# The fixed instruction order lifted from an attention and convolution mixer

## The chip, the cores and the metric

The kernel runs on one core of a Trainium2 chip. The metric is the device time of one execution in microseconds, taken as the median of several runs. The engines are named as in the profile: PE (TensorE matmuls; PEld is its weight load), DVE (VectorE), ACT (ScalarE), POOL (GpSimd), SP (SyncE). Each engine executes its own queue strictly in the order in which it was written; between engines there are semaphores.

## The reference

A decoder trunk of two layers on one sequence of 512 tokens, width 1024. Each layer is a feed-forward block, a mixer and another feed-forward block. The mixer of layer 0 is the part that this change touches. Cut to it:

```
h = h + 0.5 * swiglu_ffn(rms_norm(h, ffn1_norm[l]), ...)
h = h + hybrid_mixer(rms_norm(h, mix_norm[l]), cos, sin, ...)      # layer 0
h = h + 0.5 * swiglu_ffn(rms_norm(h, ffn2_norm[l]), ...)

def hybrid_mixer(h, cos, sin, w_in, dw_w, dw_b, ln_g, ln_b, w_out):
    proj = h @ w_in                                   # q, k, v: 512 each; u: 2 x 512
    q, k = apply_partial_rotary(q), apply_partial_rotary(k)    # 8 heads of 64
    # three dilated causal windows per head, mixed by their softmax denominators
    attn = einsum(softmax(lses), outs)
    glu = u[..., :512] * sigmoid(u[..., 512:])
    c = causal_depthwise_conv(glu, dw_w) + dw_b       # 31 taps
    c = silu(layer_norm(c, ln_g, ln_b))
    return concatenate([attn, c]) @ w_out
```

Layer 1 has a gated DeltaNet mixer instead, and all is float32.

## The kernel before

Activations lie transposed: 128 channels on the partitions, 512 tokens along a row, eight such tiles for the width. Every float32 matmul is done as three (L140 to L142, `mm3`): each operand is split into a high and a low part, and high x high, high x low and low x high are added in PSUM.

Weights come by `load_split`: SP issues the load into `raw`, ACT copies it to `whi` (L126) and writes its negative to `wlo` (L127), and POOL issues a DMA (L128) that adds the source onto `wlo`, so that `wlo` is the low part when this DMA has landed. There are four `raw` buffers and three pairs `whi`/`wlo`. The feed-forward blocks have a second form of this (L116 on ACT, L117 on DVE).

The mixer of layer 0 runs from about 393 to 697 us of the span, in this order of writing:

- Four rounds of two projections for the convolution's input. Within the first, the norm's row factors are made: `stats`, `scale` (a reciprocal root on DVE, L147 to L152), `rows` (L156 on PE, copied by ACT to `R`, L288). The angles of the rotation follow (`angles`: L751 to L757 on DVE, two Sin on ACT).
- Four quarters of the projection of V.
- `raw_rows` projects one head pair's q or k (24 matmuls; ACT copies the result to `qa`, L852, and DVE multiplies it by the cosine to `u`, L854). `rotate` swaps halves with a matmul (`tr`, L860), DVE multiplies by the sine and adds (L862, L863), ACT and DVE split into high and low (`qh`/`ql`, `kh`/`kl`; L865, L866).
- For each of four head pairs t: `scores` makes eight blocks of scores (`sc`, L881 to L883, 128 to 512 columns), DVE takes mask and maximum of each (L886), ACT the exponential (L887) and the division (L893). `values` transposes the probabilities (L913), ACT copies them to `pt` (L916), PE multiplies by V (L921). The values of head pair t-1 are written between the projections and rotations of t+1, ahead of the scores of t.
- The causal convolution runs on DVE: 4 channel tiles of 31 taps each, 124 instructions (L774, L778) of the tiles `cv`. `taps(n)` writes the next n of them at places chosen by hand: 5 at each projection, 7 at each quarter of V, 4 or 8 in `raw_rows`, 5 after the scores.
- `layer_norm` of the convolution is written in steps between the rotations, values and scores of the last head pair: sum on DVE (L926 to L928), mean by a matmul (L929), variance (L939, L942), then the scale, a Silu on ACT (L957) and a split.
- The out-projection: parts of the first three output tiles (attention's first inputs) are written ahead of the last values, the rest (`out_mm`) after them. `ahead` writes the first weights of the next feed-forward block in between, and `nxt.feed` makes the next norm's statistics and splits.

What sets the order: in most of the kernel, this mixer included, the instructions of PE, ACT and DVE are under a manual schedule, so that each of these engines executes them as written. PSUM has two banks for each of the names `mm`, `sc`, `tr`, `po`; a third score block therefore waits for the maximum of the first. The DeltaNet mixer of layer 1 is not under a manual schedule. The functions that the change touches, with the profile's line numbers:

Of the kernel before, what the change touches and what calls it, by code (L numbers as in the profile page):

```python
# [50 lines left out]
def trunk(ctx, tc, io, out, phases):  # L51
    nc = tc.nc
# [44 lines left out]
    def psum(tag):  # L97
        return pp.tile([P, T], F32, tag=tag, name=nm(tag))
# [215 lines left out]
    def step(ahead):  # L314
        if ahead is not None:
            next(ahead, None)
# [394 lines left out]
        return take, early()  # L711

    def hybrid(xn, nxt, ahead, take):
        with tc.tile_pool(name="ho", bufs=1, side="right", reuse_waits="tile") as op, \
                tc.manual_schedule(engines={nc.tensor.engine, nc.scalar.engine, nc.vector.engine}):
            with tc.tile_pool(name="hy", bufs=1, side="right", reuse_waits="tile") as hp:
                o_x, ps = hybrid_heads(xn, op, hp, take)
            xn.close()
            nxt.open()
            for d in range(NK):  # L720
                if d < 3:
                    out_mm(ps[d], take(20 + d), o_x, (4, 5, 6, 7, 3), False, True)
                else:
                    ps[d] = psum("po" if d % 2 else "mm")
                    wt = take(20 + d)
                    for _ in range((0, 0, 0, 0, 0, 0, 1, 1)[d]):
                        step(ahead)
                    out_mm(ps[d], wt, o_x, range(NK), True, True)
                V.tensor_add(h[d], ps[d], h[d])
                nxt.feed(d)  # L730
                for _ in range((0, 0, 0, 0, 0, 0, 2, 2)[d]):
                    step(ahead)
            nxt.fed()

    def out_mm(ps, wt, xs, ks, first, last):
        for k in ks:
            hi, lo = wt[k // 4]
            c = slice(k % 4 * P, k % 4 * P + P)
            mm3(ps, hi[:, c], lo[:, c], xs[k], first and k == ks[0], last and k == ks[-1])
# [614 lines left out]
    for i, ph in enumerate(phases):  # L1354
        if ph == "m_0":
            hybrid(xs[i], xs[i + 1], stages[i + 1], take)
        elif ph == "m_1":
            gdn(xs[i], xs[i + 1], stages[i + 1])
        else:
            try:  # L1360
                stages[i].send((xs[i + 1], stages[i + 1]))
            except StopIteration:
                pass
# [90 lines left out]
```

## Time and profile before

| | |
|---|---|
| median of 3 runs | 2170.47 us (2166.86 to 2171.05) |
| the profiled execution | 2171.57 us |
| its span | 2169.8 us |
| its mean granted TensorE clock | 0.961 |
| PE / DVE / ACT / POOL busy | 94% / 75% / 51% / 6% |
| the mixer of layer 0 | about 393 to 697 us of the span |

The span is the time from the first to the last instruction of one profiled execution. A row of the timeline has the start, the length, the engine, the line, the operation with its output and inputs, and in brackets how long the engine stood before it and what released it. A row of the waits has how long an engine stood for one kind of releaser in total, how often, and the longest.

### The profile page before, as it was taken

The page shows a single profiled execution, that of the slowest core. Times are in us where ns is not written, and L with a number is a line of the kernel's source. Part 1 is how long each engine was busy: PE and PEld are TensorE (multiplying, and loading weights), DVE is VectorE, ACT ScalarE, POOL GpSimd, SP SyncE. Part 2 cuts the span into 40 slices and gives each one's busy share as a digit, 9 for nine tenths or more (in the row PEclk, how much of TensorE's full clock was granted, in tenths as well). Part 3 has the DMA queues.
Part 4 walks back from the last instruction along what each step waited for, and adds up shares of the span by engine and source line. Part 5 has one row for each costly group of instructions (what it writes and reads, how often), then busy time and mean ns, then how long its engine had stood idle before and what let it go on. Part 6 is the DMA issues. An engine that isn't in the chain of part 4 may idle for free.

```text
span 2169.8 us, 32960 instructions
## 1 busy us (share of the span) xinstructions
PE 2034.5 (94%) x12694; PEld 1799.4 (83%) x12694; DVE 1624.2 (75%) x2758; ACT 1117.0 (51%) x1981; POOL 133.8 (6%) x190
## 2 busy tenths in 40 slices
PE   7999999997678999999899999998989999999997
PEld 6999997774446999997799999776778888999986
DVE  5888778786536788789888887865765568888876
ACT  5444447444444444446544445676535664444455
POOL 0000000110000000000000000033402220000000
PEclk9999999997779999999999999999979999999999
DMA  3333333772104333332233332379836453333331
GB/s 121 105 101 109 101 100 104 166 168 52 39 20 121 98 100 110 98 98 78 93 107 98 107 107 89 110 219 230 194 100 151 107 122 113 103 107 98 103 93 44
DMA packets 108845, 237.70 MB, mean 110 GB/s; under 512 B 22160, under 2 KB 24976, under 8 KB 108688
## 3 DMA queue, kind: packets, MB, share of 16 engines
q1 hardware_dynamic: 90544, 193.06, 29.0%
q0 software_dynamic: 17616, 42.02, 10.5%
q8 instruction: 99, 1.62, 0.3%
q10 hardware_dynamic: 528, 0.52, 0.1%
q14 instruction: 58, 0.48, 0.1%
HBM read 224.55 MB, written 11.01 MB: 109 GB/s over the span
## 4 chain that ended last, share of the span: by engine, by line
PE 74%; DVE 11%; issue 9%; ACT 3%; DMA 3%; POOL 0%; SPq 0%; DVEq 0%; POOLq 0%; ACTq 0%
PE mm L141 11%; PE mm L142 11%; PE mm L140 11%; PE sc L141 7%; PE sc L140 7%; PE sc L142 7%; PE po L142 2%; PE po L141 2%; PE po L140 2%; PE tr L140 2%; PE tr L142 2%; PE tr L141 2%; DVE cv L778 1%; DVE wlo L117 1%; DVE gl L386 1%
## 5 line engine op out<-in xcount | busy, mean ns | idle before, releaser
L117 DVE TENSOR_TENSOR wlo<-raw,whi 128x1024 fp32r<-128x1024 f32 (+1 forms) x400 | 473.1, 1201 | 161.0 <-ACT whi L116 156.6
L140 PE MATMUL mm<-xh,whi 128*128 128x256 f32 (+2 forms) x1800 | 562.9, 313 | 8.6 <-ACT b L456 4.0
L142 PE MATMUL mm<-xh,wlo 128*128 128x256 f32 (+2 forms) x1800 | 558.2, 310 | 7.6 <-DMA wlo<-in_whyb 4.3
L141 PE MATMUL mm<-xl,whi 128*128 128x256 f32 (+2 forms) x1800 | 557.2, 310 | 0.0
L116 ACT ACTIVATE whi<-raw 128x1024 fp32r<-128x1024 f32 (+1 forms) x400 | 404.5, 1033 | 31.1 <-issue 14.4
L140 PEld LDWEIGHTS mm<-xh,whi 128*128 128x128 f32 (+1 forms) x1800 | 344.5, 191 | 43.5 <-ACT b L456 7.2
L141 PEld LDWEIGHTS mm<-xl,whi 128*128 128x128 f32 (+1 forms) x1800 | 344.7, 191 | 26.3 <-issue 0.5
L142 PEld LDWEIGHTS mm<-xh,wlo 128*128 128x128 f32 (+1 forms) x1800 | 344.7, 192 | 24.7 <-DMA wlo<-in_whyb 5.1
L140 PE MATMUL sc<-xh,whi 128*128 128x256 f32 x1056 | 301.6, 286 | 13.2 <-ACT whi L116 5.6
L141 PE MATMUL sc<-xl,whi 128*128 128x256 f32 x1056 | 300.1, 284 | 2.2 <-DVE xl L251 2.2
L142 PE MATMUL sc<-xh,wlo 128*128 128x256 f32 x1056 | 300.3, 284 | 1.8 <-DVE wlo L117 1.7
L140 PEld LDWEIGHTS sc<-xh,whi 128*128 128x128 f32 x1056 | 203.5, 193 | 15.7 <-DVE b L458 6.2
L141 PEld LDWEIGHTS sc<-xl,whi 128*128 128x128 f32 x1056 | 203.5, 193 | 2.7 <-DVE xl L251 2.7
L142 PEld LDWEIGHTS sc<-xh,wlo 128*128 128x128 f32 x1056 | 203.6, 193 | 2.5 <-DVE wlo L117 2.5
L386 DVE TENSOR_TENSOR gl<-g,gh 128x512 fp32r<-128x512 f32 (+1 forms) x286 | 178.5, 643 | 32.3 <-ACT gh L385 29.9
L385 ACT ACTIVATE gh<-g 128x512 fp32r<-128x512 f32 (+1 forms) x286 | 166.3, 592 | 67.1 <-PE mm L141 34.7
L403 ACT ACTIVATE a<-a 128x512 f32<-128x512 f32 x88 | 55.6, 632 | 253.9 <-DVE a L402 253.9
L442 ACT ACTIVATE b<-mm 128x256 f32<-128x256 f32 x84 | 32.1, 383 | 155.9 <-PE mm L142 155.9
L126 ACT ACTIVATE whi<-raw 128x512 fp32r<-128x512 f32 (+2 forms) x109 | 76.7, 732 | 58.8 <-PE mm L141 36.5
L456 ACT ACTIVATE b<-mm 128x256 f32<-128x256 f32 x88 | 33.6, 382 | 139.5 <-PE mm L142 139.5
L778 DVE SCALAR_TENSOR_TENSOR cv<-pad,prm_t,cv 128x512 f32<-128x512 f32 x120 | 90.1, 751 | 4.1
L141 PE MATMUL mm<-gl,whi 128*128 128x512 f32 (+1 forms) x220 | 83.0, 377 | 4.8 <-DVE gl L386 4.6
(419 smaller groups left out, 3567.2 us busy)
## 6 DMA issues: line engine op xcount, KB each, us to landing
raw<-in_wf1i SPq DMA_DIRECT2D x82, 512.0 KB, 3.5
raw<-in_wf2i SPq DMA_DIRECT2D x82, 512.0 KB, 3.5
raw<-in_wgdn SPq DMA_DIRECT2D x32, 512.0 KB, 4.2
wlo<-in_wgdn POOLq DMA_DIRECT2D x64, 256.0 KB, 6.0
raw<-in_wf2i SPq DMA_DIRECT2D x56, 256.0 KB, 2.6
raw<-in_wf1i SPq DMA_DIRECT2D x52, 256.0 KB, 2.6
raw<-in_wf1b SPq DMA_DIRECT2D x20, 512.0 KB, 3.5
raw<-in_wf2b SPq DMA_DIRECT2D x20, 512.0 KB, 3.5
```

What stands on the lines that cost most here:

```text
L116: A.activation(hi[:, s], src[:, s], AF.Copy)
L117: V.tensor_sub(lo[:, s], src[:, s], hi[:, s].bitcast(F32))
L126: A.activation(hi[:, s], raw[:, s], AF.Copy)
L140: PE.matmul(ps, whi, xhi, start=first, stop=False, skip_group_check=skip)
L141: PE.matmul(ps, whi, xlo, start=False, stop=False, skip_group_check=skip)
L142: PE.matmul(ps, wlo, xhi, start=False, stop=last, skip_group_check=skip)
L385: A.activation(hi, g[f][:, s], AF.Copy)
L386: V.tensor_sub(lo, g[f][:, s], hi.bitcast(F32))
L403: A.activation(cg[f], cg[f], AF.Silu)
L442: A.activation(b0[f][:, HT:], pb[f][:, :HT], AF.Copy)
L456: A.activation(b1[f][:, :HT], pb[f][:, :HT], AF.Copy)
L778: V.scalar_tensor_tensor(acc, x, w, acc, op0=ALU.mult, op1=ALU.add)
```

## The change

The `hybrid` function enters two contexts: a pool, and the manual schedule for the three engines. The second is dropped; the scheduler now orders the instructions of the mixer on these engines, from the same written sequence. The feed-forward blocks stay under their manual schedules.

```
     def hybrid(xn, nxt, ahead, take):
-        with tc.tile_pool(name="ho", bufs=1, side="right", reuse_waits="tile") as op, \
-                tc.manual_schedule(engines={nc.tensor.engine, nc.scalar.engine, nc.vector.engine}):
+        with tc.tile_pool(name="ho", bufs=1, side="right", reuse_waits="tile") as op:
             with tc.tile_pool(name="hy", bufs=1, side="right", reuse_waits="tile") as hp:
                 o_x, ps = hybrid_heads(xn, op, hp, take)
```

From this line on, line numbers are one lower than before. Each engine has the same instructions; on PE 284 change their place, on DVE 315, on ACT 163, on POOL none, and on SP two pairs of loads swap.

VectorE, from the last score maximum of head pair 0 to the rotation behind it. `cv` are convolution taps, `tr_799` is the swapped key of head pair 1, `rd` a reciprocal of the softmax's denominators. Before:

```order
L886 ISA s3_790_4848,m_791_4849<-sc_789_4844,hcst_4054 128x512
L886 ISA m_791_4849 128x1
L891 RECIPROCAL rd_767_4782<-den_765_4780 128x4
L778 SCALAR_TENSOR_TENSOR cv_747_4704<-pad_684_4258,prm_t_67,cv_747_4704 128x512 x13
L854 TENSOR_TENSOR u_798_4905<-mm_796_4870,Ct_653_4060 128x512
L862 TENSOR_TENSOR t1_800_4909<-tr_799_4907,St_654_4061 128x512
L863 TENSOR_TENSOR u_759_4768<-u_759_4768,t1_800_4909 128x512
L866 TENSOR_TENSOR kl_802_4913<-u_759_4768,kh_801_4912 128x512
```

And now:

```order
L885 ISA s3_790_4846,m_791_4847<-sc_789_4842,hcst_4052 128x512
L885 ISA m_791_4847 128x1
L777 SCALAR_TENSOR_TENSOR cv_813_4971<-pad_695_4338,prm_t_67,cv_813_4971 128x512 x3
L890 RECIPROCAL rd_767_4780<-den_765_4778 128x4
L861 TENSOR_TENSOR t1_800_4907<-tr_799_4905,St_654_4059 128x512
L853 TENSOR_TENSOR u_798_4903<-mm_796_4868,Ct_653_4058 128x512
L862 TENSOR_TENSOR u_759_4766<-u_759_4766,t1_800_4907 128x512
L777 SCALAR_TENSOR_TENSOR cv_813_4971<-pad_695_4338,prm_t_67,cv_813_4971 128x512 x2
L865 TENSOR_TENSOR kl_802_4911<-u_759_4766,kh_801_4910 128x512
```

Thirteen taps stood between the maximum and the rotation, and three stand there now; they are of the fourth channel tile (`cv_813`) instead of the third, since the earlier ones are already done. Ahead of these rows, taps of two tiles alternate in the new order, where a tile's taps followed each other before. Counted up to the first score maximum of head pair 0, 78 of the 124 taps stood ahead before and 99 now; between the last row of the first rotated key (`kl_753`) and that maximum there were eight taps, and there are four. All 124 stand ahead of the rotated key of head pair 2 (`kl_866`) now, and the LayerNorm sum (L926) stands among the scores of head pair 2 instead of behind them.

TensorE at the scores of head pair 0. `sc_768`, `sc_771`, `sc_774`, `sc_777` are the first four score blocks, `mm_796` the projection of the next query. Before:

```order
L881 MATMUL sc_771_4791<-kh_752_4722,qh_741_4668 128x256
L882 MATMUL sc_771_4791<-kl_753_4723,qh_741_4668 128x256
L883 MATMUL sc_771_4791<-kh_752_4722,ql_742_4669 128x256
L881 MATMUL sc_774_4799<-kh_752_4722,qh_741_4668 128x384
L882 MATMUL sc_774_4799<-kl_753_4723,qh_741_4668 128x384
L883 MATMUL sc_774_4799<-kh_752_4722,ql_742_4669 128x384
L881 MATMUL sc_777_4807<-kh_752_4722,qh_741_4668 128x512
```

And now:

```order
L882 MATMUL sc_771_4789<-kh_752_4720,ql_742_4667 128x256
L140 MATMUL mm_796_4868<-xh_512_3534,whi_744_4672 128x512
L141 MATMUL mm_796_4868<-xl_513_3535,whi_744_4672 128x512
L142 MATMUL mm_796_4868<-xh_512_3534,wlo_745_4673 128x512
L140 MATMUL mm_796_4868<-xh_522_3573,whi_744_4672 128x512
L141 MATMUL mm_796_4868<-xl_523_3574,whi_744_4672 128x512
L142 MATMUL mm_796_4868<-xh_522_3573,wlo_745_4673 128x512
L140 MATMUL mm_796_4868<-xh_538_3630,whi_744_4672 128x512
L141 MATMUL mm_796_4868<-xl_539_3631,whi_744_4672 128x512
L880 MATMUL sc_774_4797<-kh_752_4720,qh_741_4666 128x384
```

The eight score blocks followed each other, and then came the 24 matmuls of the projection; now eight of these stand behind the second block, four behind the fourth, two behind the sixth, and ten behind the last. The transposes of the probabilities (L913, now L912) are interleaved with the next projection in the same way: two of its matmuls behind the first group, six behind the second. In head pairs 2 and 3 parts of the out-projection take the projection's place.

ScalarE at the out-projection's first weight (`whi_981`, `wlo_982`). Before:

```order
L893 ACTIVATE s3_974_5511<-s3_974_5511,rd_951_5445 128x512
L952 ACTIVATE t1_978_5526<-tr_977_5521 128x512
L126 ACTIVATE whi_981_5535<-raw_980_5533 128x1024
L127 ACTIVATE wlo_982_5536<-whi_981_5535 128x1024
L957 ACT_TABLE_LOAD
L957 ACTIVATE cv_677_4209<-cv_677_4209,prm_t_67 128x512
```

And now:

```order
L915 ACTIVATE pt_872_5172<-tr_871_5169 128x256
L126 ACTIVATE whi_981_5533<-raw_980_5531 128x1024
L851 ACTIVATE qa_877_5218<-mm_876_5185 128x512
L127 ACTIVATE wlo_982_5534<-whi_981_5533 128x1024
L915 ACTIVATE pt_884_5236<-tr_883_5231 128x512
```

It stood behind the last divisions of the last head pair, and now stands among the copies of the transposed probabilities two head pairs earlier, 51 instructions before. At the front, DVE's angles (L750 to L756 now) alternate with the reciprocal root, eight more matmuls of the second projection stand ahead of the transposes of the row factors on PE, the two Sin ahead of the copy to `R` on ACT, and the splits of the second round's weights (`whi_680`) ahead of the gate's tanh. At the end, the splits of the last output tiles' weights and of the next feed-forward block's first weights stand ahead of the squares and splits of `nxt.feed`.

## The prediction

> **What bounds the kernel now.** First the page: where the span ends and who fills it.
>
> ```profile
> span 2169.8 us, 32960 instructions
> PE 2034.5 (94%) x12694; PEld 1799.4 (83%) x12694; DVE 1624.2 (75%) x2758; ACT 1117.0 (51%) x1981; POOL 133.8 (6%) x190
> ...
> L778 DVE SCALAR_TENSOR_TENSOR cv<-pad,prm_t,cv 128x512 f32<-128x512 f32 x120 | 90.1, 751 | 4.1
> ```
>
> TensorE (PE) sets the end of the span, and an average of 94% leaves 135 us in which it stood. The change touches one phase of six, so I looked next at the stretches of that phase, busy time and granted clock side by side.
>
> ```profile
> 425.00:479.00 54.00, 54.00 (x236) 44.17 (x235) 40.14 (x56) 24.11 (x27) 7.77 (x9) 0.99 0.79 177
> 479.00:650.00 171.00, 122.86 (x427) 81.63 (x426) 93.05 (x191) 78.43 (x164) 5.18 (x6) 0.75 0.18 41
> 650.00:700.00 50.00, 39.80 (x171) 31.41 (x170) 33.33 (x54) 25.20 (x30) 4.32 (x5) 0.95 0.44 95
> ```
>
> The columns are length, then busy time of PE, PEld, DVE, ACT and POOL, then the granted clock. While the projections run (425 to 479) PE is full at clock 0.99, one matmul every 0.23 us (54.00 / 236), and VectorE (DVE) has 13.9 us free. In the attention part (479 to 650) PE stands 171 - 122.86 = 48.1 us, and its busy time runs at 0.75: 122.86 x 0.25 = 30.7 us lost to the clock, 92.1 us of work at full speed. No engine is full there; the stretch is made of waits. The waits of PE from 393 to 720 name them (total, times, longest):
>
> ```profile
> PE sc L881 <- DVE m L886: 14.3, 7, 8.8
> PE tr L913 <- DVE t L862: 10.3, 4, 4.9
> PE sc L929 <- DVE t L928: 7.3, 1, 7.3
> PE tr L913 <- ACT pt L916: 6.9, 9, 1.2
> PE sc L140 <- ACT whi L116: 5.6, 1, 5.6
> PE sc L142 <- DMA wlo<-in_whybo: 5.1, 1, 5.1
> PE mm L142 <- DMA wlo<-in_whyb: 4.3, 2, 4.1
> PE tr L942 <- DVE t L939: 4.2, 1, 4.2
> PE po L142 <- DMA wlo<-in_whybo: 3.5, 1, 3.5
> PE sc L142 <- DVE wlo L117: 1.0, 1, 1.0
> ```
>
> Rows 1 to 4, 6 and 8 add up to 48.1, the whole idle time of 479 to 650. The front has 4.3, the out-projection 3.5, the next phase's start 5.6 + 1.0.
>
> **The change, part by part.** No instruction is added or removed; three engines run the same ones in another order. So every term is a wait that shrinks, grows or appears.
>
> *Scores of head pair 0 and the second rotation.* The rows of DVE, and PE beside them:
>
> ```profile
> 485.72 6.26 DVE L778 SCALAR_TENSOR_TENSOR cv<-pad,prm_t,cv 128x512 f32<-128x512 f32 x8
> 491.90 0.68 DVE L854 TENSOR_TENSOR u<-mm,Ct 128x512 f32<-128x512 f32 x1
> 492.50 0.68 DVE L862 TENSOR_TENSOR t<-tr,St 128x512 f32<-128x512 f32 x1
> ...
> 495.56 0.68 PE L881 MATMUL sc<-kh,qh 64*128 64x384 f32 x1 [8.76 <-DVE m L886]
> ...
> 504.31 10.17 DVE L778 SCALAR_TENSOR_TENSOR cv<-pad,prm_t,cv 128x512 f32<-128x512 f32 x13
> 514.40 0.68 DVE L854 TENSOR_TENSOR u<-mm,Ct 128x512 f32<-128x512 f32 x1
> ...
> 515.73 1.11 PE L913 MATMUL tr<-cst,s 128*128 128x128 f32 x4 [4.04 <-DVE t L862]
> ```
>
> Eight convolution taps in a row stand ahead of the rotation and the first score maximum, and PE waits 8.76 us for the maximum to free a score bank. In the new order four of those taps stand there: 4 x 0.78 = 3.1 us earlier. Eight matmuls of the next projection, 1.8 us at 0.23 each, fill part of the rest. All told 99 taps instead of 78 are done by then, 21 x 0.75 = 15.8 us more work, but DVE has that room earlier (13.9 us free in 425 to 479 alone, some 3 us around it) and its taps now alternate between two channels: 13 chained taps took 10.17 (0.78 each), while neighbours that don't depend on each other started 0.60 apart (491.90 to 492.50). Of that 0.18 I count 0.115 for each of some 50 taps, since a tap lasts 0.07 longer than those neighbours: 6 us, of which about 2.5 land on this wait. So 8.76 - 3.1 - 1.8 - 2.5 = 1.3 us remain; bounds 0 and 8.8. The other six of the seven (5.5 us) I cut to a third, 1.8, since matmuls of the projection stand between the score blocks there too: 14.3 becomes 3.1.
>
> Thirteen taps then hold up the rotation that PE waits 4.04 for (4.9 in the next head pair). Three stand there now: ten fewer, 7.8 us, more than the wait. Each drops to about 0.5; with the two small ones 10.3 becomes 2.0. VectorE's queue behind the taps (the score maxima, and ScalarE's exponentials that wait for them) comes forward with it.
>
> PE's nine waits on ScalarE for transposed probabilities (L916), of at most 1.2 us each, are covered by matmuls of the next projection that now stand between the transposes: two or more at 0.23 each time, and six behind the second group. 6.9 becomes 1.9.
>
> The Trainium skill, "VectorE: DVE Perf Modes", section "The DRAIN you can't avoid", has it that the next operation starts only when the pipeline has emptied and that leaving out semaphores gains nothing; by that, alternating channels saves none of the 6 us and the forecast would be 6 us higher. The trace shows 0.78 against 0.60 apart, so it disagrees for these shapes.
>
> *The convolution's LayerNorm.*
>
> ```profile
> 585.35 3.08 DVE L778 SCALAR_TENSOR_TENSOR cv<-pad,prm_t,cv 128x512 f32<-128x512 f32 x4
> 588.35 0.68 DVE L926 TENSOR_TENSOR t<-cv,cv 128x512 f32<-128x512 f32 x1
> ...
> 590.54 2.08 PE L929 MATMUL sc<-t,hcst 128*128 128x512 f32 x2 [7.29 <-DVE t L928]
> ```
>
> The last four taps stand behind all scores, and PE waits 7.29 for the sum. They are now done before the scores of that head pair, the sum inside them: 0. The variance's 4.2 falls to 0.3 with it.
>
> *The tail and the weights of the out-projection.*
>
> ```profile
> 626.51 1.92 ACT L893 ACTIVATE s<-s,rd 128x128 f32<-128x128 f32 x4 [0.25 <-DVE rd L891]
> ...
> 628.81 1.05 ACT L126 ACTIVATE whi<-raw 128x1024 fp32r<-128x1024 f32 x1
> ...
> 630.97 1.28 ACT L957 ACT_TABLE_LOAD   x1
> ...
> 631.24 0.86 POOL L128 DMA_DIRECT2D wlo<-in_whybo  x1 [70.05 <-ACT wlo L127]
> ...
> 632.26 0.81 ACT L957 ACTIVATE cv<-cv,prm_t 128x512 f32<-128x512 f32 x1
> 633.11 0.63 ACT L134 ACTIVATE hi<-cv 128x512 fp32r<-128x512 f32 x1
> ...
> 636.44 0.79 PE L142 MATMUL sc<-hi,wlo 128*128 128x512 f32 x1 [5.08 <-DMA wlo<-in_whybo]
> ```
>
> ScalarE splits this weight at 628.81, POOL's DMA follows and lands 5.2 us after its issue. The split now stands 51 instructions earlier, two score blocks ahead, so the 5.1 us go. POOL's and SP's queues carry nothing else at that time (0.86 us of issue), so moving the transfer collides with nothing. In exchange PE has already done the parts of the out-projection that filled this place, and comes earlier to the first part that needs the convolution's output. That part waits for normalising, table load, Silu and split: 1.92 + 1.28 + 0.81 + 0.63 = 4.6 plus small steps, bounds 0 and 5.2; I take 4.3, near the whole chain, since nothing is left to put there. The scores of the last head pair now start as soon as their keys are rotated: a chain like 492.50 to 495.56 (3.1 us), of which I take 1.8, and 1.2 for the next two score blocks, bounds 0 and 4.9 (the longest wait for a rotation now). New waits: 7.3.
>
> *Front.* The angles of the rotation (L751 to L757) are now interleaved with the reciprocal root that the row factors need:
>
> ```profile
> 398.53 0.42 DVE L751 CAST qa<-qa 128x512 f32<-128x512 int32 x1
> ...
> 402.61 0.43 DVE L757 TENSOR_SCALAR qa<-qa 128x512 f32<-128x512 f32 x1
> ```
>
> They take 4.5 us, and at worst all of that goes in front of the factors. Eight matmuls of the second projection now stand ahead of the factors' transposes on PE and hide 1.8; one of the two Sin ahead of the factors' copy on ScalarE adds 0.6 (a 128x512 activation, as at 633.11). I take 4.5 - 1.8 + 0.6 = 3.3 of new wait. Against it the weights' splits stand ahead of that chain on ScalarE and the 4.3 of the wait for a weight's DMA go: a gain of 1.0, bounds -4.5 and +4.3.
>
> *Out-projection and start of the next phase.* The remaining weight splits stand ahead of the feed's squares and splits on ScalarE. 3.5 becomes 2.1 and 5.6 + 1.0 becomes 1.0, a gain of 7.0, bounds 0 and 10.1.
>
> *The clock.*
>
> ```profile
> 495.00:508.00 13.00, 11.93 (x33) 9.48 (x34) 7.76 (x24) 11.02 (x27) 0.00 (x0) 0.52 0.00 1
> 534.00:546.00 12.00, 10.97 (x40) 8.25 (x39) 6.89 (x23) 9.49 (x26) 0.00 (x0) 0.72 0.00 1
> 576.00:591.00 15.00, 6.96 (x26) 5.22 (x26) 9.65 (x26) 9.12 (x25) 0.00 (x0) 0.61 0.00 0
> ...
> 535.97 0.44 PE L881 MATMUL sc<-kh,qh 64*128 64x384 f32 x1 [0.74 <-DVE m L886]
> ```
>
> The clock is low after the long waits, but also in 534 to 546, where the longest wait was 0.74. So I don't give back all of the 30.7: in proportion to the idle time that is left. That is 3.1 + 2.0 + 1.9 + 0.3 + 7.3 = 14.6 of 48.1, or 30%: 9.3 stay lost, 21.4 are gained. The Trainium skill, "TensorE: Matmul & The Clock Gate", section "HAM oscillation — how this bites in real kernels", puts half clock down to idle gaps longer than about 3.4 us; only one wait of that size would be left, and by that rule nearly all 30.7 come back (the second rival's time).
>
> **Sum.** 1.0 (front) + 33.5 (48.1 - 14.6) + 21.4 (clock) + 7.0 = 62.9. The profiled execution took 2171.57 us (span 2169.8 and 1.8 around it): 2108.7. It lies 1.1 above the median of the runs, 2170.47, so I predict 2107.6.
>
> **The rivals.** *VectorE becomes the bound.*
>
> ```profile
> 398.00:588.30 190.30, 154.98 (x599) 114.27 (x597) 137.57 (x233) 85.80 (x148) 15.54 (x18) 0.86 0.45 102
> ```
>
> Up to the LayerNorm sum it is busy 137.57 of 190.3 us, 72%. My sum needs some 38 of the gains before 588, so about 90% busy without the alternation, 86% with it. If it reaches only 80%, the sum comes at 570 instead of 588: 18.0, and behind it 3.9 + 2.3 + 5.1 + 7.0 - 5.5 = 12.8. That gives 2171.57 - 30.8 - 1.1 = 2139.7. For it speaks that taps still precede score maxima in an engine that runs in order.
>
> *The clock comes back whole.* If matmuls that follow each other closely are enough to hold 0.99 here as in 425 to 479, the 9.3 are gained too: 2098.3; with the new waits at their lower bounds some 7 less, 2091. Against it speaks 534 to 546.
>
> *Slower: the clock stays down.* The new order puts small score and transpose matmuls (64 rows, 128 to 512 columns) between the projection's full ones, so there may be no stretch left that restores the clock. The 92.1 us of work plus 14.6 of waits, less 8.0 from front and end, equal today's 171 at clock 92.1 / 164.4 = 0.56; below that the change costs. At the 0.52 of 495 to 508 it gives 92.1 / 0.52 + 14.6 - 8.0 - 171 = 12.7 more: 2183. Against it: the projections hold 0.99.
>
> *Nothing measurable.* Waits taken away on PE could reappear behind DVE's taps, since the taps are only moved; that needs every term to be paid back, and would give 2170.
>
> **Chances.** The forecast (2100 to 2115) 0.40, VectorE bound or half of the gain (2115 to 2155) 0.28, the clock whole (2082 to 2100) 0.16, slower 0.12, nothing 0.04. A difference under 0.2% (4.3 us) can't be told from none on this kernel. Range 2082 to 2150, which leaves out the last two and the far end of the second; faster 0.84, same 0.04, slower 0.12.
>
> **What would show it.** In the new profile: the waits of L880 for the maximum and of L912 for L861 below 1.5 us each; no wait of L928; a wait of 2 to 5 us of the out-projection's matmul for the Silu's split; granted clock about 0.9 in the attention stretch; DVE near 90% busy from 400 on. Wrong would be: DVE late at the first maximum, the clock at 0.75 with few waits, or a PE wait well over 3.3 us on the row factors around 398, which would mean that the angles weigh more than taken.

## The result and the profile after

The changed kernel takes 2098.93 us (median of 3 runs, 2097.34 to 2100.03), against 2170.47: ratio 0.9674, 95% interval 0.9652 to 0.9696. The prediction was 2107.6, in a range of 2082 to 2150. The profiled execution has a span of 2097.2 us, 72.6 less than before.

The page after, where the span ends and who fills it:

```profile
span 2097.2 us, 32970 instructions
...
PE 2020.4 (96%) x12694; PEld 1785.7 (85%) x12694; DVE 1609.0 (77%) x2758; ACT 1113.9 (53%) x1981; POOL 134.0 (6%) x190
```

To compare the two traces I cut them at the same instructions of PE: the statistics of the mixer's norm (L271), the first score matmul, and the first matmul of the next phase. The two stretches of before, and then those of after; the columns are length, busy time of PE, PEld, DVE, ACT and POOL, and the granted clock:

```profile
392.53:485.85 93.32, 88.66 (x384) 71.21 (x382) 73.37 (x115) 39.72 (x45) 12.09 (x14) 0.98 0.73 164
485.85:690.77 204.92, 153.22 (x558) 106.08 (x557) 112.65 (x225) 97.25 (x187) 9.50 (x11) 0.79 0.23 52
```

```profile
390.90:479.34 88.44, 86.81 (x383) 70.15 (x381) 85.89 (x143) 41.62 (x48) 13.07 (x15) 1.00 0.79 184
479.34:621.78 142.44, 138.28 (x557) 91.33 (x557) 90.72 (x200) 92.90 (x187) 8.64 (x10) 0.93 0.32 71
```

The front became 4.9 us shorter, the stretch from the scores through the out-projection 62.5 us. The rest is 3.6 us behind it and 1.6 us in the unchanged first phase (the same instructions end there at 390.90 instead of 392.53; in the traces of the kernels below that have the same first phase they lie anywhere between 390.5 and 392.8, so this part can't be put down to the change). Together that is the 72.6. In the long stretch PE's idle time went from 51.7 to 4.2 us, its busy time from 153.2 to 138.3 and its clock from 0.79 to 0.93. VectorE shows where its work went: 12.5 us more of it in the front, 21.9 us less behind.

The waits of PE from 479 to 650 in the changed kernel, to be read against the ten rows of before:

```profile
PE mm L140 <- ACT hi L134: 1.2, 1, 1.2
PE sc L141 <- DVE xl L251: 1.1, 1, 1.1
PE po L142 <- DMA wlo<-in_whybo: 1.0, 1, 1.0
...
PE sc L880 <- ACT kh L864: 0.7, 1, 0.7
...
PE sc L880 <- DVE m L885: 0.5, 2, 0.3
...
PE tr L912 <- ACT pt L915: 0.2, 1, 0.2
```

The score maximum (14.3 before) is down to 0.5, the rotation, the LayerNorm sum and the variance aren't in the list any more, and among the new waits are the two that were named: the Silu's split (1.2) and the last rotated key (0.7). At the start of the next phase the 5.6 + 1.0 for a weight have become 1.1 + 0.5 for the split of that phase's input (`xl`, `xh`).

VectorE's timeline at the first scores:

```profile
476.85 2.73 DVE L777 SCALAR_TENSOR_TENSOR cv<-pad,prm_t,cv 128x512 f32<-128x512 f32 x4
479.50 0.68 DVE L861 TENSOR_TENSOR t<-tr,St 128x512 f32<-128x512 f32 x1
480.10 0.68 DVE L853 TENSOR_TENSOR u<-mm,Ct 128x512 f32<-128x512 f32 x1
480.69 0.68 DVE L862 TENSOR_TENSOR u<-u,t 128x512 f32<-128x512 f32 x1
481.29 0.28 DVE L885 CUSTOM_DVE_ANT_0 s<-sc,hcst 128x128 f32<-128x128 f32 x1
...
482.51 0.68 DVE L865 TENSOR_TENSOR ql<-u,qh 128x512 fp32r<-128x512 f32 x1
```

The first maximum starts at 481.29, 1.95 us after the first score matmul (479.34). Before it was 9.4 us after it (495.21 against 485.85). Before, all of the next query's rotation stood ahead of the maxima, its split (L866) included; now the split stands behind two of them.

### The profile page after: what moved, and what is told of

Read it like the earlier page. It is cut to its first block, busy times and chain, and to the rows that moved or that the text cites. A ratio compares the mean times of both kernels' runs of the same rounds, so it can differ in the third digit from the quotient of the medians.

```text
span 2097.2 us, 32970 instructions
## 1 busy us (share of the span) xinstructions
PE 2020.4 (96%) x12694; PEld 1785.7 (85%) x12694; DVE 1609.0 (77%) x2758; ACT 1113.9 (53%) x1981; POOL 134.0 (6%) x190
## 4 chain that ended last, share of the span: by engine, by line
PE 80%; DVE 8%; issue 5%; ACT 3%; DMA 3%; SPq 0%; POOL 0%; DVEq 0%; ACTq 0%; POOLq 0%
PE mm L141 13%; PE mm L140 13%; PE mm L142 13%; PE sc L141 7%; PE sc L140 7%; PE sc L142 7%; PE po L142 3%; PE po L141 2%; PE po L140 2%; PE tr L140 2%; PE tr L142 2%; PE tr L141 2%; DVE wlo L117 1%; DVE gl L386 1%; PE tr L1051 1%
## 5 line engine op out<-in xcount | busy, mean ns | idle before, releaser
L117 DVE TENSOR_TENSOR wlo<-raw,whi 128x1024 fp32r<-128x1024 f32 (+1 forms) x400 | 473.3, 1201 | 158.8 <-ACT whi L116 154.3
L116 ACT ACTIVATE whi<-raw 128x1024 fp32r<-128x1024 f32 (+1 forms) x400 | 404.8, 1034 | 33.9 <-issue 14.4
L777 DVE SCALAR_TENSOR_TENSOR cv<-pad,prm_t,cv 128x512 f32<-128x512 f32 x120 | 83.8, 743 | 0.8
```

Source lines behind the costliest of these rows:

```text
L116: A.activation(hi[:, s], src[:, s], AF.Copy)
L117: V.tensor_sub(lo[:, s], src[:, s], hi[:, s].bitcast(F32))
L777: V.scalar_tensor_tensor(acc, x, w, acc, op0=ALU.mult, op1=ALU.add)
```

## The experiments

**Which engine's order is it?** The manual schedule takes a set of engines, so that it can be kept or lifted for each one. The edit, here for the first run; the others name other engines:

```
-                tc.manual_schedule(engines={nc.tensor.engine, nc.scalar.engine, nc.vector.engine}):
+                tc.manual_schedule(engines={nc.tensor.engine}):
```

TensorE fixed, the other two free:

> TensorE keeps its order of before, VectorE and ScalarE are ordered by the scheduler. Theory (most of the gain is VectorE's taps and ScalarE's weight splits coming out of the way, the fill on TensorE is worth little): the waits of 8.8, 4.0, 4.9, 7.3 and 5.1 us of before all fall below 3 us, the small waits on transposed probabilities (6.9 us) stay; time 2105 to 2120. Rival (it is TensorE's interleaving that fills the waits): the waits named stay above half of their size; time 2135 to 2160.

VectorE fixed, the other two free:

> VectorE keeps its order of before, TensorE and ScalarE are ordered by the scheduler. Theory (VectorE's order makes the waits): TensorE still waits for the score maximum (5 to 9 us), the rotations (4 us each) and the LayerNorm sum (7 us or more, since TensorE comes there earlier); only the weight waits go (5.1 + 3.5 + 6.6 + 4.3 with the clock); time 2140 to 2160. Rival (TensorE's interleaving fills the waits): 2105 to 2125.

ScalarE fixed, the other two free:

> ScalarE keeps its order of before, TensorE and VectorE are ordered by the scheduler. Theory: the weight waits of 5.1, 3.5 and 5.6 us and the 4.1 us in the front come back, and since TensorE now reaches some weights earlier, one or two of them are longer than before; the waits on VectorE stay gone; time 2115 to 2130. Rival (ScalarE's order is a by-product that costs nothing): within 5 us of the changed kernel, 2095 to 2105.

VectorE alone free:

> Only VectorE is ordered by the scheduler; TensorE and ScalarE keep their order of before. Theory: the 8.8 falls to some 3 us, the rotations' 4.0 and 4.9 and the sum's 7.3 go, the weight waits and the 6.9 stay; some 20 us less idle time and 12 us of clock; time 2130 to 2142. Rival (the engines' new orders need each other, one alone gains nothing): 2160 to 2175.

ScalarE alone free:

> Only ScalarE is ordered by the scheduler; TensorE and VectorE keep their order of before. Theory: the waits for weights go (5.1, 5.6, 4.1 and part of 3.5 us, with some 5 us of slow clock behind them), all waits on VectorE stay; time 2148 to 2156. Rival (a weight that comes earlier only moves the wait to VectorE's next step): 2163 to 2173.

TensorE alone free:

> Only TensorE is ordered by the scheduler; VectorE and ScalarE keep their order of before. Theory: the small waits on transposed probabilities (6.9 us) and part of the first wait go, but TensorE now stands in front of work whose inputs VectorE and ScalarE deliver late, above all the out-projection parts that were moved up; time 2150 to 2175. Rival (TensorE's interleaving is the gain): 2105 to 2130.

What came out (ratio to the kernel before on the same chip, 95% interval):

| free engines | us | ratio |
|---|---|---|
| none (before) | 2172.3 and 2172.2 | 1 |
| VectorE | 2130.49 | 0.9803 (0.9773 to 0.9833) |
| ScalarE | 2151.08 | 0.9906 (0.9884 to 0.9929) |
| TensorE | 2160.43 | 0.9948 (0.9931 to 0.9965) |
| VectorE + ScalarE | 2110.52 | 0.9706 (0.9677 to 0.9735) |
| VectorE + TensorE | 2114.66 | 0.9730 (0.9695 to 0.9765) |
| ScalarE + TensorE | 2143.02 | 0.9859 (0.9831 to 0.9887) |
| all (the change) | 2098.93 | 0.9674 (0.9652 to 0.9696) |

Five of the six times fell within the bounds of the theory, and the one with ScalarE fixed 0.3 us below them. The three single gains, 2.0%, 0.9% and 0.5%, add up to 3.4%; all together give 3.3%. VectorE's order carries more than half of it: 60% when it alone is lifted, and 57% is lost when it alone is kept. For ScalarE these shares are 29% and 17%, for TensorE 16% and 10%; the two kernels with one of them kept (0.9730 and 0.9706) aren't clear of each other.

The sum comes out although the gains aren't independent, as two places show. The front is won by either of two engines: with VectorE alone free it is 88.95 us long, with ScalarE alone free 88.05, against 93.32 before and 88.44 with all free, so adding the single gains counts it twice. The start of the next phase needs both: with VectorE alone free the wait for ScalarE's split (L116) is still 4.1 us, and with ScalarE alone free that wait is 1.0, but TensorE then waits 5.9 us for VectorE's part of the same weight (L117). With both free neither is left, and the longest wait there is 1.1. There the rival of that run was right, although its time wasn't.

Why TensorE alone gains little is seen in its waits:

```profile
PE mm L140 <- DVE u L854: 17.5, 2, 9.7
PE sc L929 <- DVE t L928: 6.1, 1, 6.1
PE sc L140 <- ACT whi L116: 5.6, 1, 5.6
PE mm L140 <- ACT hi L134: 4.0, 3, 2.7
```

The wait for the score maximum is gone from the top, but as a wait for `u` (L854): the projection that was moved between the scores needs a `mm` bank, and VectorE frees it only behind its taps. With ScalarE free as well it is the same: 10.1 us for `u`, and not the waits for the maximum and the LayerNorm sum that were expected. With VectorE alone free, the longest waits are other engines' deliveries:

```profile
PE tr L913 <- ACT pt L916: 9.2, 6, 3.0
PE sc L142 <- DMA wlo<-in_whybo: 4.7, 1, 4.7
PE sc L140 <- ACT whi L116: 4.1, 1, 4.1
PE sc L881 <- DVE m L886: 3.9, 7, 0.8
```

The seven waits for a maximum are 3.9 us in all, without any projection matmul between the scores; the weights of the out-projection and of the next phase are ScalarE's part, and the transposed probabilities (6.9 before, 9.2 here) TensorE's.

**Which part of the program is it?** The fixed order kept for all three engines, but only over a part of the mixer. The front:

```
+        front = ExitStack()
+        front.enter_context(tc.manual_schedule(engines={...}))
         K.update(consts_in(hp, "hcst", HCONSTS))
...
             vt.append(v)
+        front.close()
```

> The fixed order holds for the front (the convolution's input projections and V), and the scheduler orders the rest. The front's 4.9 us of gain are lost in any case. Theory: taps can be moved only out of the attention part's own supply, so VectorE enters it with the taps of before (about 50 done at its start instead of some 75), and a wait of several us for the score maximum or a rotation comes back; time 2110 to 2125. Rival (the attention part has room enough on VectorE for the taps): 2101 to 2108.

2104.29 us, ratio 0.9688 (0.9667 to 0.9709), within the bounds of the rival. Its front is 91.4 us long (88.4 in the changed kernel), with the wait for a weight's DMA at 3.4, and the stretch behind is 144.3 against 142.4. Only 90 taps are done at the first maximum, not 99, and no wait for VectorE over 1.1 us comes back.

The second part of the out-projection:

```
             nxt.open()
+            tail = ExitStack()
+            tail.enter_context(tc.manual_schedule(engines={...}))
             for d in range(NK):
...
             nxt.fed()
+            tail.close()
```

> The fixed order holds for the second part of the out-projection (the loop over its eight output tiles), and the scheduler orders all before it. Theory: ScalarE has its weight splits behind the feed again, 3.5 us in the out-projection and 5.6 + 1.0 us at the start of the next phase return; time 2104 to 2110. Rival (that start is decided by something else): 2097 to 2101.

2107.50 us, but the runs lie from 2098.34 to 2115.06 (ratio 0.9701, 0.9666 to 0.9735), so the time doesn't separate the two. The trace, which is of the slowest of the four runs, shows 3.3 us on a weight's DMA in the out-projection and 5.5 + 1.0 us at the start of the next phase back, as the theory had it.

**What in VectorE's order is it?** First the places of the taps, by hand, in the kernel before with its fixed order:

```
-                taps(5)
+                taps(6)
...
-            taps(7)
+            taps(11)
...
-        k = raw_rows(13, 4)
+        k = raw_rows(13, 11)
...
-                q = raw_rows(14 + 2 * t, 8)
+                q = raw_rows(14 + 2 * t, 8 if t else 4)
...
-                k = raw_rows(15 + 2 * t, 8)
+                k = raw_rows(15 + 2 * t, 9 if t else 4)
...
-            taps(5)
             qr = qn
```

> The kernel before, in its fixed order on all three engines; only the numbers of taps at each place are changed so that as many are done at each point as the scheduler's order has (36 and 44 instead of 30 and 28 in the projections, 99 instead of 78 at the first score maximum, 4 instead of 8 right ahead of it, none behind the scores). Taps of one channel tile still follow each other. Theory (the place of the taps is the gain, their alternation between tiles a detail worth up to 6 us): 2130 to 2142, as VectorE's order alone gave 2130.5. Rival (without alternation VectorE has no room for the earlier taps, and TensorE waits for it in the projections or at the first maximum): 2145 to 2165.

2164.51 us, ratio 0.9962 (0.9946 to 0.9978). The theory fell: a fifth of what VectorE's own order gave. VectorE was busy for 43.05 of the 45 us from 440 to 485, and its first maximum came at 498.95, later than the 495.21 of before. The two stretches, front and from the scores through the out-projection, show where it was lost:

```profile
390.87:492.03 101.16, 90.87 (x383) 72.19 (x382) 90.69 (x139) 38.89 (x45) 12.11 (x14) 0.97 0.67 148
492.03:685.01 192.98, 150.95 (x557) 104.69 (x557) 95.02 (x201) 97.88 (x187) 9.50 (x11) 0.81 0.26 56
```

Fewer taps behind the first scores made the second stretch 11.9 us shorter than before (204.92), and more of them ahead made the front 7.8 us longer (93.32). So the alternation of tiles, which I had called a detail, was the next suspect. The same kernel with a conv generator that takes taps in turn from the two oldest unfinished tiles:

```
+                    i, j = live.pop(0)
+                    V.scalar_tensor_tensor(cv[i], pads[i][:, j:j + T], dwh[:, i * 31 + j:i * 31 + j + 1],
+                                           cv[i], op0=ALU.mult, op1=ALU.add)
+                    if j < 29:
+                        live.append([i, j + 1])
                yield
```

> As the kernel with the taps moved by hand (fixed order on all engines, 99 taps ahead of the first score maximum), but successive taps now alternate between the two oldest channel tiles that aren't finished. In the traces so far a tap that follows its own tile's tap starts 0.785 us after it, and one that follows another tile's 0.66 us. Theory (the alternation is what makes room on VectorE): 99 x 0.12 = 12 us earlier at the first maximum than without it, the waits of TensorE for VectorE fall below 2 us each; 2132 to 2145. Rival (the other moves in VectorE's order, rotations and split ahead of the taps, are what counts): 2155 to 2165.

2156.62 us, ratio 0.9913 (0.9887 to 0.9939), within the bounds of the rival. The alternation is worth 8 to 12 us here (7.9 between the medians, 12.5 between the spans of the traces). The two stretches of this kernel, and those of the one with VectorE alone free:

```profile
392.75:487.63 94.88, 88.43 (x384) 71.16 (x382) 84.39 (x139) 38.90 (x45) 12.10 (x14) 0.98 0.71 158
487.63:674.50 186.87, 147.23 (x557) 103.47 (x558) 93.76 (x201) 97.95 (x187) 9.51 (x11) 0.83 0.27 58
```

```profile
391.01:479.96 88.95, 86.93 (x383) 70.06 (x381) 83.84 (x141) 41.59 (x47) 13.01 (x15) 1.00 0.77 172
479.96:652.72 172.76, 146.92 (x558) 102.70 (x558) 92.78 (x200) 94.82 (x184) 9.26 (x11) 0.85 0.28 60
```

VectorE's timeline at the first scores, with the taps by hand and alternating:

```profile
488.22 2.73 DVE L777 SCALAR_TENSOR_TENSOR cv<-pad,prm_t,cv 128x512 f32<-128x512 f32 x4
490.87 0.68 DVE L855 TENSOR_TENSOR u<-mm,Ct 128x512 f32<-128x512 f32 x1
491.47 0.68 DVE L863 TENSOR_TENSOR t<-tr,St 128x512 f32<-128x512 f32 x1
492.18 0.69 DVE L864 TENSOR_TENSOR u<-u,t 128x512 f32<-128x512 f32 x1
493.57 0.69 DVE L867 TENSOR_TENSOR ql<-u,qh 128x512 fp32r<-128x512 f32 x1 [0.70 <-ACT qh L866]
494.18 0.28 DVE L887 CUSTOM_DVE_ANT_0 s<-sc,hcst 128x128 f32<-128x128 f32 x1
```

Its taps were where the scheduler has them and alternated as there (four in 2.73 us), and still the maximum waits: it stands behind the whole rotation of the next query, which the written order puts first, and in that rotation VectorE stands 0.70 us for ScalarE's part. The kernel with VectorE alone free has its first maximum at 481.05, ahead of that rotation's second half:

```profile
480.45 0.68 DVE L862 TENSOR_TENSOR t<-tr,St 128x512 f32<-128x512 f32 x1
481.05 0.28 DVE L886 CUSTOM_DVE_ANT_0 s<-sc,hcst 128x128 f32<-128x128 f32 x1
481.25 0.08 DVE L886 DVE_READ_ACCUMULATOR2_ANT m<- 128x1 f32 x1
481.25 0.69 DVE L863 TENSOR_TENSOR u<-u,t 128x512 f32<-128x512 f32 x1
...
482.69 0.69 DVE L866 TENSOR_TENSOR ql<-u,qh 128x512 fp32r<-128x512 f32 x1
```

The two kernels have the same number of taps ahead to within two (97 and 99), and are 26 us apart: 14.1 in the stretch from the scores on, 5.9 in the front, the rest outside both. VectorE also comes to the first scores late in the alternating kernel: its last row for them, `kl` (L867), starts at 487.61, just ahead of the first score matmul (487.63), while in the changed kernel it starts at 476.24, 3.1 us ahead (479.34). Last, the changed kernel with alternation made impossible:

```
+                if t:
+                    V.scalar_tensor_tensor(acc, x, w, cv[t - 1], op0=ALU.mult, op1=ALU.add)
+                else:
                     V.tensor_scalar(acc, x, w, pr["dwb"][:, t:t + 1], op0=ALU.mult, op1=ALU.add)
```

> The changed kernel, its order free, but the first tap of each channel tile adds the tile before instead of the bias, so that no tile can begin before the one ahead is finished and taps can't alternate (the convolution's values are others than the reference's). Theory (alternation makes the room): some 90 taps fewer alternate, 90 x 0.12 = 11 us more on VectorE up to the LayerNorm sum, of which the attention part, where VectorE has some 20 us free, hides about half; 2103 to 2115. Rival (a scheduler that places the taps freely hides them whole): 2097 to 2102.

2100.79 us, ratio 0.9663 (0.9641 to 0.9685), not to be told from the changed kernel (0.9652 to 0.9696). Where the order is free, 88 taps ahead of the first maximum do as well as 99: the others go into gaps between later maxima, and the LayerNorm sum starts at 541.67 instead of 529.95 without anyone waiting over 1.0 us for it. So neither the number of early taps nor their alternation carries the gain by itself. What the runs leave is the rest of VectorE's order: a maximum or a rotation stands first in the queue when its input is there, and taps fill what is between. No run changed that alone with everything else fixed, so it is inferred from the two kernels above and not shown, and its share is open: their 26 us also hold the front, and whatever else differs in VectorE's order.

**What lowers the clock?** The changed kernel still runs at half clock for some 17 us, with no wait over 0.73 us in the 30 us before:

```profile
545.00:550.00 5.00, 4.04 (x20) 2.65 (x20) 3.62 (x10) 4.14 (x11) 0.00 (x0) 1.00 0.00 0
550.00:555.00 5.00, 5.00 (x20) 3.38 (x20) 2.04 (x12) 2.86 (x9) 0.00 (x0) 0.54 0.00 0
555.00:560.00 5.00, 5.00 (x11) 2.10 (x9) 0.61 (x5) 0.19 (x2) 0.00 (x0) 0.50 0.00 0
560.00:565.00 5.00, 5.00 (x15) 3.22 (x15) 2.09 (x7) 3.12 (x8) 0.00 (x0) 0.50 0.00 0
```

So I measured kinds of matmul by themselves; the block was put behind the first norm's feed:

```
+            full(60)
+            ps = psum("sc")
+            for _ in range(60):
+                PE.matmul(ps, zw[:64], zx[:64], start=True, stop=True)
...
+            for n in (1, 3):
+                for _ in range(14):
+                    ps = psum("sc")
+                    for _ in range(n):
+                        PE.matmul(ps, zw, zx, start=True, stop=True)
+                    A.activation(zx, ps, AF.Copy, scale=0.05)
```

> The changed kernel with a block of extra matmuls behind the first norm's feed, whose results nothing uses: stretches of some 14 to 25 us of one kind, each followed by 60 full matmuls (128 rows, 128 columns, 512 wide): 60 with 64 rows; 24 float32 ones with 64 columns; 120 transposes of 128x128 in float32; 100 of 128x1; then 14 rounds of one full matmul that waits for ScalarE's copy of the one before (gaps near 1 us), and 14 rounds of three. Time: about 200 us more, without meaning. Theory (the clock follows how much of the array the matmuls of the last microseconds use, not long gaps): granted clock near 0.5 in at least the rounds with 1 us gaps and in one or more of the small kinds (128x1 above all), although no gap is over 1.5 us. Rival (only a gap of 3.4 us or so brings it down): 1.00 in every stretch.

The time (2332.27 us, one run) has no meaning. The stretches, in order: 64 rows, 64 columns, transposes, 128x1 (its second half), one matmul per round, three per round:

```profile
54.00:68.00 14.00, 14.00 (x62) 11.00 (x60) 0.00 (x0) 0.00 (x0) 0.00 (x0) 1.00 0.00 1
81.80:102.60 20.80, 20.80 (x50) 6.50 (x49) 0.00 (x0) 0.00 (x0) 0.00 (x0) 1.00 0.00 0
116.30:129.30 13.00, 13.00 (x120) 12.96 (x119) 0.00 (x0) 0.00 (x0) 0.00 (x0) 1.00 0.00 1
163.00:183.40 20.40, 20.40 (x97) 20.40 (x97) 0.00 (x0) 0.00 (x0) 0.00 (x0) 0.50 0.00 1
208.00:217.80 9.80, 5.03 (x7) 1.72 (x6) 0.00 (x0) 4.18 (x7) 0.00 (x0) 0.50 0.00 0
236.00:247.00 11.00, 6.49 (x21) 3.40 (x21) 0.00 (x0) 3.58 (x6) 0.00 (x0) 1.00 0.00 1
```

Half the rows or half the columns, back to back, don't lower the clock. Back-to-back 128x1 matmuls do, with PE busy all the time, and so does one full matmul per round, whose gaps are 0.7 us. Three per round, with gaps just as long (0.75), keep it at 1.00. So the length of a gap doesn't decide it here. The theory, that the clock follows how much of the time the array streams columns, fits these rows; no run separates it from other measures of the array's work, and each kind was measured once. The Trainium skill, "TensorE: Matmul & The Clock Gate", section "HAM oscillation — how this bites in real kernels", speaks of idle gaps over about 3.4 us; these two stretches fall to 0.50 without one. The 128x1 matmuls of the LayerNorm's variance stand just ahead of the 17 slow us in the changed kernel, at 549.57, after score blocks with small waits between them; which of them tips it was not tried.

## Why the prediction was right

- **The sum** (62.9 us) was 8.6 us short of the 71.5 between the medians. The traces: front 4.9 (predicted 1.0), attention and out-projection 62.5 (predicted 33.5 + 21.4 + 1.4 = 56.3), behind it 3.6 (5.6), and 1.6 in a phase that is the same in both. The mechanism behind most of it, waits of PE for the other engines' queues that go, is what the traces show. That the 56.3 lies so near the 62.5 is in part luck, since two misses work against each other: PE's idle time fell by 47.5 us in that stretch (51.7 to 4.2), 12.6 more than the 33.5 + 1.4 of the sum, and its busy time by 14.9 (153.22 to 138.28), 6.5 less than the 21.4 that the clock was to give.
- **Front, mis-sized.** The stall on the row factors is 1.14 + 0.49 us instead of 3.3. And I had left out that after its wait of 4.1 us PE ran slowly: a weight that comes in time saves that too (busy time 88.66 to 86.81). I put this gain down to ScalarE's splits. ScalarE alone free did give the whole of it, a front of 88.1 us, but so did VectorE alone free, nearly, with 89.0.
- **Idle time, right in kind.** 16.7 us were to be left in the stretch (14.6, and 2.1 in the out-projection), and 4.2 are. The new wait for the Silu's split is 1.2 instead of 4.3, that for the last key 0.7 instead of 1.8 + 1.2. In both places I had PE stand for most of a chain, while the scheduler kept other matmuls for that time: parts of the out-projection, transposes and values.
- **The first maximum: right in its result, wrong in its parts.** 8.8 was to fall to 1.3 by 3.1 (fewer taps right ahead), 1.8 (matmuls that fill) and 2.5 (alternation). It fell to at most 0.3. VectorE's order alone, without the fill, brings this wait to at most 0.8, and the same taps by hand, alternating, leave 5.3. The part that I did not name, the maximum ahead of the next query's rotation, is what the runs leave as the reason, together with VectorE's coming there earlier. The pace itself was as taken: 0.78 us for a tap behind its own tile's (26 taps in 20.35 us, 439.82 to 460.17, with the taps by hand), 0.66 behind another's (7 in 4.64 us, 424.26 to 428.90, in the changed kernel), 0.12 apart. By the Trainium skill, "VectorE: DVE Perf Modes", section "The DRAIN you can't avoid", as I had read it, such an alternation saves nothing, and here it saves 0.12 us a tap. My reading was too narrow: the same section says that an operation which is not held starts earlier.
- **The LayerNorm sum and the weights** went as described: 7.3 to nothing, 5.1 to nothing, 3.5 to 1.0.
- **The clock: a matching number for a wrong reason.** 9.3 us were to stay lost, and 138.28 x 0.07 = 9.7 did by the mean clock. But the loss was not in proportion to the idle time: nearly all of it lies in one stretch of 17 us with hardly any wait. And the clock's 21.4 did not all arrive, since PE's busy time fell by 14.9. Where the other 6.5 went wasn't measured. TensorE's new order itself is one candidate: with it kept as before and the other two engines free, the stretch has 136.78 us of busy time at a lower clock (0.91), against 138.28 at 0.93.
- **The rivals.** VectorE did become full where it was feared: 85.89 of 88.44 us in the front, but the free order lets maxima and rotations pass the taps, so that nobody waits. (The 2139.7 of that rival can't be traced whole: the 2.3 us in it has no row.) The clock came back to 0.93, not whole. The slower case, a clock held down by chopped matmuls, did not come: the interleaved stretch from 480 to 540 has 1.00. The chopping does cost a little: behind a score matmul the second projection matmul starts 0.33 us after the first (480.23 to 480.56), and the next ones 0.24 and 0.23 apart.

```profile
480.02 0.28 PE L882 MATMUL sc<-kh,ql 64*128 64x256 f32 x1
480.23 0.50 PE L140 MATMUL mm<-xh,whi 128*128 128x512 f32 x1
480.56 0.40 PE L141 MATMUL mm<-xl,whi 128*128 128x512 f32 x1
480.80 0.40 PE L142 MATMUL mm<-xh,wlo 128*128 128x512 f32 x1
```

## What to carry to other kernels

In an engine that executes in order, look first at what stands ahead of the instruction that another engine waits for: here a rotation not yet needed and a filler stood ahead of a score maximum, and moving filler by count alone recovered a fifth of what a free order of that engine did, since it lengthened the front by 7.8 us while it shortened the rest by 11.9. Lift or keep a fixed order for one engine at a time: it shows whose queue makes the waits. Look at the stretches too, and not only at the total: the parts added up here although one gain was to be had from either of two engines and another only from both. The speed of the filler was worth 8 to 12 us in the fixed order, and nothing that could be measured in the free one.

## What the hardware showed

In one run, the granted clock fell to 0.50 with PE busy all the time (128x1 matmuls) and with gaps of only 0.7 us (one 512-wide matmul in 1.2 to 1.5 us), and stayed at 1.00 with gaps of 0.75 us when three matmuls stood between them. Half the rows, half the columns or 128-wide transposes back to back did not lower it.
